# Seven block products for eight in a gate/up projection, on one core

## The chip, the cores and the metric

The kernel runs on one core of a Trainium2 chip. The metric is the device time of one execution in microseconds (us). Three runs of the kernel before took 954.88, 955.64 and 956.01 us; the median is 955.64 us.

## The reference

The kernel computes one decoder layer on x of 512 tokens by 1024 channels in float32: a SwiGLU block, a mixing block (attention and a state space model) and a second SwiGLU block, each between two RMS norms and added to x. The change lies in the last block:

```python
def swiglu(x, w_in, w_out):
    gate, up = jnp.split(x @ w_in, 2, axis=-1)
    return (jax.nn.silu(gate) * up) @ w_out
...
        h = rms_norm(x, ffn2_pre_g[l])
        x = x + 0.5 * rms_norm(swiglu(h, ffn2_w_in[l], ffn2_w_out[l]), ffn2_post_g[l])
```

w_in is 1024 x 5632 (2816 gate columns, then 2816 up columns) and w_out 2816 x 1024.

## The kernel before

The layer runs in three parts (f, m, g in `run`): the first SwiGLU, the mix, the second SwiGLU. Between two parts `boundary` closes the one and opens the next.

Float32 products are made of three matmuls. Each operand is split in a high part of type float32r and a rest: ScalarE casts (L102 for weights, L148 for results), VectorE or GpSimd subtracts (L104, L149). `mm3` multiplies high by high, high by rest and rest by high. All matmuls stand at L129.

In SwiGLU the 2816 hidden columns are 22 tiles f of 128. x lies transposed in SBUF, channels on partitions: `x` unscaled, and `xh`, `xl` times the gain of the norm before. For tile f `products(f)` loads the gate chunk and the up chunk (1024 x 128 each, 512 KB, one DMA on SP's queue into `wraw`), splits each into `whi` and `wlo` (four buffers each; the gate's rest on VectorE, the up's on GpSimd) and runs 8 x 3 matmuls with 512 token columns into a PSUM bank `gu`. `hidden(f)` multiplies both banks by the norm's factor `r` on VectorE (L400, L402), applies Silu to the gate on ScalarE (L401), multiplies (L403) and splits the result into `ah`, `al` at place f % 8 (L148, L149). Tiles 0 and 1 are opened by `boundary` in banks `first`, with matmuls of 256 columns.

In the second SwiGLU `outp_tokens(i)` multiplies six tiles with w_out after tiles 6, 12 and 18, into `yo` banks and then `y`, tokens on partitions; the last four tiles wait for `finish`, with their weights in `tw`, loaded while tiles 18 to 21 run. `finish` multiplies them (`yt`), adds, takes the norm and adds the old x, which `tokens_first` has turned to tokens on partitions by TensorE transposes and kept in SBUF as `xt`. Four token blocks b of 128 are finished in the order 0, 1, 2, 3, the last in three parts.

TensorE runs its matmuls in the order in which the program is written (`fix`); what isn't fixed on the other engines is put in order by the scheduler. Each engine then works off its own row of instructions in order. PSUM has eight banks.

The order of the second SwiGLU around the change:

```python
        for f in range(NF):
            if f >= nfirst:
                products(f)
...
            if last and f in (6, 12, 18):
                outp_tokens(f // 6 - 1)
```

Of the kernel before, what the change touches and what calls it, by code (L numbers as in the profile page):

```python
# [12 lines left out]
ALU = mybir.AluOpType  # L13
# [12 lines left out]
FLAST = ((0, 6), (6, 6), (12, 6))  # L26
QOFF = (0, 128, 384, 768, 1280)
RING = 8
HT = S // 2
H = 8  # L30
E = 64
# [9 lines left out]
class Layer:  # L41
# [323 lines left out]
    def ffn_chunks(self, w_in):  # L365
        return [w_in[c] for c in (0, NF, 1, NF + 1)]

    def ffn(self, n, first, scope, params):
        nc = self.nc
        last = not params  # L370
        w_in, w_out, w_tail = (self.a[n + t] for t in "iot")
        early = scope.enter_context(ExitStack())
        hook = self.tokens_first(scope) if last else self.ssm_params(early)
        o0, _, r, late = first
        if not last:
            y = self.ktiles("y")
# [8 lines left out]
        if self.ahead:  # L385
            between = {(nfirst, 0): {}, (nfirst, 1): {6: lambda: late[0](fixp=self.fix)}, (nfirst + 1, 0): {6: late[1]}}
        else:
            between = {(nfirst, 0): {5: late[0]}, (nfirst, 1): {2: late[1]}}

        def products(f):  # L390
            o[f] = []
            for i, c in enumerate((f, NF + f)):
                w = self.ahead.pop(0) if self.ahead else self.load(w_in[c], (KD, P), pool=i == 1)
                b = self.bank("gu")
                self.mmk(b, w, self.xh, self.xl, hooks=between.get((f, i), other[i]))
                o[f].append(b)

        def hidden(f):
            gt, ut = self.tmp("gt"), self.tmp("ut")
            nc.vector.tensor_tensor(out=gt, in0=o[f][0], in1=r, op=ALU.mult)  # L400
            nc.scalar.activation(out=gt, in_=gt, func=AF.Silu)  # L401
            nc.vector.tensor_tensor(out=ut, in0=o[f][1], in1=r, op=ALU.mult)  # L402
# [16 lines left out]
        def outp_tokens(i):  # L419

            f0, nf = FLAST[i]
            for d in range(2):
                b4 = [self.bank("yo") for _ in range(4)]
                for k in range(nf):
                    if k % 2 == 0:
                        wh, wl = self.load(w_out[(f0 + k) // 2, d], (2, S), pool=k % 4 == 2)
                    s = (f0 + k) % RING
                    for b in range(4):
                        ts = slice(b * P, (b + 1) * P)
                        self.mm3(b4[b], ah(s)[:, ts], al(s)[:, ts], wh[:, k % 2], wl[:, k % 2], k == 0, k == nf - 1)  # L430
                for b in range(4):
                    if i == 0:
                        nc.scalar.copy(out=y(b, d), in_=b4[b])
                    else:
                        nc.vector.tensor_tensor(out=y(b, d), in0=b4[b], in1=y(b, d), op=ALU.add)

        for f in range(NF):
            if f >= nfirst:
                products(f)
            if f == lag:  # L440
                for i in range(lag):
                    hidden(i)
            if f >= lag:
                hidden(f)
            if last and f == 6:
                for _ in hook:
                    pass
                yk = self.ktiles("y")
                y = lambda b, d: yk(2 * b + d)
            if last and f in (6, 12, 18):  # L450
                outp_tokens(f // 6 - 1)
            if not last and f in (7, 14):
                outp(f // 7 - 1)
            if f == NF - NT:
                for _ in hook:
                    pass
                early.close()
                tp = scope.enter_context(self.tc.tile_pool(name="bd" + n, bufs=1))
            if f >= NF - NT:
                self.load_tail(tp, w_tail, f - (NF - NT), f % 2 == 1)  # L460
        tail = lambda k: (ah((NF - NT + k) % RING), al((NF - NT + k) % RING))
        if last:
            return self.finish(y, tail)
        outp(2)
        return y, tail

    def tokens_first(self, scope):

        nc = self.nc
        pool = scope.enter_context(self.tc.tile_pool(name="fin", bufs=1))  # L470
        xt = self.ktiles("xt")
        self.xt = lambda b, d: xt(2 * b + d)
        self.gt = pool.tile([P, 2, S], F32, name="gt")
        nc.sync.dma_start(out=self.gt.rearrange("p d c -> p (d c)"), in_=self.a["glast"].to_broadcast([P, D]))
        for b in range(4):
            for d in range(2):
                yield
                o = self.bank("xt")
                for k in range(4):
                    nc.tensor.transpose(o[:, k * P:(k + 1) * P], self.x(4 * d + k)[:, b * P:(b + 1) * P], self.ident)  # L480
                nc.scalar.copy(out=self.xt(b, d), in_=o)

    def finish(self, y, tail):


        nc, V, fx = self.nc, self.nc.vector, self.fix
# [5 lines left out]
        parts = lambda b: ((0, S), (S, S)) if b < 3 else ((0, S), (S, HT), (S + HT, HT))  # L492
        cols = lambda c, n: (c // S, slice(c % S, c % S + n))

        def product(b, i, k0=0, k1=NT):
# [17 lines left out]

        def gain(b, i):
            d, sl = cols(*parts(b)[i])
            yg[b, i] = self.wp.tile([P, S], F32, name="yg", tag=("whi", "wlo")[b % 2], bufs=4)[:, :parts(b)[i][1]]
# [12 lines left out]

        def final(b, i):  # L530
            c, n = parts(b)[i]
            fx(V.scalar_tensor_tensor(out=yg[b, i], in0=yg[b, i], scalar=rs[:, b:b + 1], in1=at(self.xt, b, i),
                                      op0=ALU.mult, op1=ALU.add))
            fx((nc.scalar if i == 1 else nc.sync).dma_start(out=self.a["out"][b * P:(b + 1) * P, c:c + n], in_=yg[b, i]))

        early = [(0, 0), (0, 1)]
        for b, i in early:
            product(b, i, 0, NT - 1)
        for b, i in early:
            product(b, i, NT - 1)  # L540
        for b in range(1, 4):
            for i in range(len(parts(b))):
                product(b, i)
        for b in range(3):
            for i in range(2):
                gather(b, i)
                gain(b, i)
                add_sum(b, i)
                if i == 0 and b:
                    final(b - 1, 0)  # L550
                    final(b - 1, 1)
        final(2, 0)
        for i in range(2):
            gather(3, i)
            gain(3, i)
        add_sum(3, 0)
        add_sum(3, 1)
        gather(3, 2)
        gain(3, 2)
        add_sum(3, 2)  # L560
        final(2, 1)
        for i in range(3):
            final(3, i)


    def ssm_params(self, scope):
# [599 lines left out]
    def run(self, parts="fmg"):  # L1166
# [5 lines left out]
        for p, q in zip(parts, parts[1:] + " "):  # L1172
            with ExitStack() as scope:
                if p == "m":
                    out = self.mix(first, scope)
                else:
                    out = self.ffn("w1" if p == "f" else "w2", first, scope, p == "f")
                if p != "g":
                    first = self.boundary(*out, *post[p], *nxt[q])

# [66 lines left out]
```

## Time and profile before

| | us |
|---|---|
| median of three runs | 955.64 |
| span of the profiled execution, first to last instruction | 951.7 |
| own time of the profiled execution | not given apart from its span |
| second SwiGLU, from its first matmul to the last one of `finish` | 602.1 to 944 |
| one transfer of 512 KB of w_in from issue to landing (median of 44) | 3.5 |

The span is that of one execution; the runs' median is 3.9 us longer than it, for what lies around the instructions. TensorE's clock was granted at 0.998 on average. In the views below PE is TensorE, PEld its weight loads, DVE VectorE, ACT ScalarE, POOL GpSimd and SP the engine whose queue issues most transfers. In the chain, each row is a piece of work that had to end before the next could start; in the groups, the number behind the bar is the busy time, then the mean time of one.

### The profile page before, as it was taken

Reading aid. Unit: us, or ns where it says so; the run is one execution under the profiler, and the core shown is the slowest. Engines: PE = TensorE matmul, PEld = TensorE weight load, DVE = VectorE, ACT = ScalarE, POOL = GpSimd, SP = SyncE. Lnnn points to the kernel's source line nnn. Section 1 sums busy time; section 2 is a strip of 40 time slices with the busy share of each in tenths; the row PEclk is TensorE's granted clock in tenths of the full one; section 3 lists DMA queues with packets and bytes.
Section 4 is the critical chain, followed back from the end, with each engine's and each line's share of the span. In section 5 each row is a group of like instructions: output and inputs, shape, how many; then the busy total and the mean of one; then the engine's idle time right before and its main releaser. Section 6 shows DMA issues by size and latency. Waiting matters only on the chain.

```text
span 951.7 us, 12868 instructions
## 1 busy us (share of the span) xinstructions
PE 940.0 (99%) x5082; PEld 787.6 (83%) x5082; DVE 527.2 (55%) x934; ACT 367.2 (39%) x610; POOL 225.8 (24%) x134
## 2 busy tenths in 40 slices
PE   9999999999999999999999999999999999999996
PEld 7888888888888889978777899888888888888885
DVE  7998214463255545758897659644134524544327
ACT  7354334352234233525746545443332312223312
POOL 0234222322223233500000035421222222222301
PEclk9999999999999999999999999999999999999999
DMA  7233334353334241282323430323223223233202
GB/s 268 88 111 98 102 111 144 119 177 103 109 112 133 67 155 46 90 224 92 114 68 116 150 110 1 114 86 106 94 93 107 88 89 109 90 111 126 96 1 89
DMA packets 38173, 102.48 MB, mean 108 GB/s; under 512 B 7616, under 2 KB 10944, under 8 KB 37568
## 3 DMA queue, kind: packets, MB, share of 16 engines
q1 hardware_dynamic: 36528, 98.02, 32.0%
q10 hardware_dynamic: 1584, 3.63, 1.0%
q8 instruction: 40, 0.66, 0.3%
q14 instruction: 21, 0.17, 0.1%
HBM read 94.03 MB, written 7.60 MB: 107 GB/s over the span
## 4 chain that ended last, share of the span: by engine, by line
PE 94%; DVE 3%; ACT 1%; issue 1%; DMA 0%; SPq 0%; POOLq 0%; POOL 0%; DVEq 0%; ACTq 0%
PE gu L129 47%; PE yo L129 21%; PE yt L129 6%; PE first L129 6%; PE prj L129 3%; PE prv L129 2%; PE mo L129 2%; PE st L129 1%; PE ys L129 1%; PE gl L129 1%; PE pt L839 1%; PE sc L129 1%; PE pv L129 1%; ACT whi L102 1%; PE rp L129 0%
## 5 line engine op out<-in xcount | busy, mean ns | idle before, releaser
L104 POOL TENSOR_TENSOR wlo<-wraw,whi 128x1024 fp32r<-128x1024 f32 (+2 forms) x62 | 158.5, 2556 | 497.4 <-ACT whi L102 497.3
L102 ACT CAST whi<-wraw 128x1024 fp32r<-128x1024 f32 (+5 forms) x157 | 154.6, 991 | 302.0 <-PE gu L129 121.6
L129 PE MATMUL gu<-xh,whi 128*128 128x512 f32 x656 | 257.6, 393 | 0.0
L129 PE MATMUL gu<-xh,wlo 128*128 128x512 f32 x656 | 255.7, 390 | 0.5 <-DVE wlo L104 0.5
L129 PE MATMUL gu<-xl,whi 128*128 128x512 f32 x656 | 255.3, 389 | 0.0
L104 DVE TENSOR_TENSOR wlo<-wraw,whi 128x1024 fp32r<-128x1024 f32 (+5 forms) x95 | 113.6, 1202 | 121.5 <-ACT whi L102 121.0
L129 PEld LDWEIGHTS gu<-xh,wlo 128*128 128x128 f32 x656 | 123.1, 188 | 26.8 <-DVE wlo L104 1.0
L129 PEld LDWEIGHTS gu<-xh,whi 128*128 128x128 f32 x656 | 123.2, 188 | 25.4 <-issue 0.4
L129 PEld LDWEIGHTS gu<-xl,whi 128*128 128x128 f32 x656 | 123.2, 188 | 25.1
L402 DVE TENSOR_TENSOR ut<-gu,rs 128x512 f32<-128x512 f32 x41 | 28.2, 689 | 102.9 <-PE gu L129 102.8
L149 DVE TENSOR_TENSOR al<-ut,ah 128x512 fp32r<-128x512 f32 x44 | 67.1, 1527 | 25.4 <-ACT ah L148 25.4
L400 DVE TENSOR_TENSOR gt<-gu,rs 128x512 f32<-128x512 f32 x41 | 28.2, 689 | 50.7 <-PE gu L129 50.7
L129 PE MATMUL yo<-ah,whi 128*128 128x512 f32 x144 | 56.0, 389 | 0.0
L129 PE MATMUL yo<-al,whi 128*128 128x512 f32 x144 | 56.0, 389 | 0.0
L129 PE MATMUL yo<-whi,ah 128*128 128x512 f32 x144 | 56.0, 389 | 0.0
L129 PE MATMUL yo<-wlo,ah 128*128 128x512 f32 x144 | 56.0, 389 | 0.0
L129 PE MATMUL yo<-whi,al 128*128 128x512 f32 x144 | 56.0, 389 | 0.0
L129 PE MATMUL yo<-ah,wlo 128*128 128x512 f32 x144 | 56.0, 389 | 0.0
L148 ACT CAST ah<-ut 128x512 fp32r<-128x512 f32 x44 | 27.2, 621 | 62.1 <-DVE ut L403 62.1
L129 PE MATMUL first<-xh,whi 128*128 128x256 f32 (+1 forms) x144 | 43.3, 301 | 0.2 <-ACT xh L151 0.2
L129 PE MATMUL first<-xl,whi 128*128 128x256 f32 (+1 forms) x144 | 42.7, 296 | 0.6 <-DVE xl L152 0.6
L129 PE MATMUL first<-xh,wlo 128*128 128x256 f32 (+1 forms) x144 | 42.5, 295 | 0.0
(194 smaller groups left out, 1406.3 us busy)
## 6 DMA issues: line engine op xcount, KB each, us to landing
wraw<-w2i SPq DMA_DIRECT2D x44, 512.0 KB, 3.5
wraw<-w1i SPq DMA_DIRECT2D x42, 512.0 KB, 3.4
wraw<-w2o SPq DMA_DIRECT2D x18, 512.0 KB, 3.4
wraw<-w1o SPq DMA_DIRECT2D x16, 448.0 KB, 3.4
wraw<-wmi SPq DMA_DIRECT2D x12, 512.0 KB, 3.7
x<-xT SPq DMA_DIRECT2D x8, 256.0 KB, 4.0
w1d<-w1s SPq DMA_DIRECT2D x8, 256.0 KB, 2.7
w2d<-zb SPq DMA_DIRECT2D x2, 1024.0 KB, 4.9
```

The source lines that it names most:

```text
L102: fix(self.nc.scalar.copy(out=hi, in_=raw))
L104: fix(eng.tensor_tensor(out=lo, in0=raw, in1=hi.bitcast(F32), op=ALU.subtract))
L129: i = self.nc.tensor.matmul(*a, **k)
L148: fix(nc.scalar.copy(out=hi, in_=src))
L149: fix(nc.vector.tensor_tensor(out=lo, in0=src, in1=hi.bitcast(F32), op=ALU.subtract))
L400: nc.vector.tensor_tensor(out=gt, in0=o[f][0], in1=r, op=ALU.mult)
L402: nc.vector.tensor_tensor(out=ut, in0=o[f][1], in1=r, op=ALU.mult)
L839: self.fix(nc.tensor.transpose(b[i][:, o:o + P], sc[:, c:c + P], self.ident))
```

## The change

Tiles 0 to 5 of the second SwiGLU stay as they are. Tiles 6 to 21 are taken in eight pairs (f, f + 1). For a pair, the weights are a 2 x 2 matrix of blocks: a11 and a12 are the gate columns of both tiles by the first and the second half of the channels, a21 and a22 the up columns. x is a 2 x 2 matrix b of channel halves by token halves. Every block product has 2 x 4 x 3 matmuls with 256 token columns. Instead of eight block products, seven are made, with sums of blocks: P1 = a11 b11, P2 = a12 b21, P3 = c2 n2, P4 = c1 n1, P5 = c3 t3, P6 = c2' b22 and P7 = a22 t4, where c3 = a11 + a21, c2 = c3 + a22, c1 = a21 + a22 and c2' = c2 + a12 are sums of weights, made for each pair on VectorE, and n1, n2, t3, t4 are signed sums of x, made once (`sums`) and split once (`plain` and `sums`). P1, P3, P5 and P7 add up in one bank (`wx`); ScalarE copies it after P1 (s1) and after P3 (s2). P2 goes to `wy`, P4 and P6 to `wq`, copied after P4 (q). Sums of these give the gate and the up halves; minus signs are put in with the last products (L602).

For the sums x must carry the norm's factors, so `sums` scales it in place; the copy of the old x therefore goes to DRAM (`xd`) and is read again in `finish`. `outp(0)` now follows tile 5; `outp(1)` and `outp(2)` follow the pairs that start at tiles 10 and 16. The weights of the last four tiles are loaded behind the last pair in the program. The last pair is split by token halves, second half first, and `finish` takes the blocks in the order 2, 3, 0, 1.

```diff
+NSTD = 6
+BLOCKS = (2, 3, 0, 1)
...
+                t = self.tmp("xt")
+                nc.scalar.copy(out=t, in_=o)
+                nc.sync.dma_start(out=self.xd[b, :, d], in_=t)
...
+        def sums():
+            for k in range(KD):
+                V.scalar_tensor_tensor(out=self.x(k), in0=self.x(k), scalar=self.g(4, k), in1=r, op0=ALU.mult, op1=ALU.mult)
+            b = lambda i, j: quarter(self.x, i, j)
+            n1, n2 = wsum(), wsum()
+            V.tensor_tensor(out=v4(n1), in0=b(0, 0), in1=b(0, 1), op=ALU.subtract)
+            V.scalar_tensor_tensor(out=v4(n2), in0=v4(n1), scalar=-1.0, in1=b(1, 1), op0=ALU.mult, op1=ALU.subtract)
+            self.split(*tq[0], n2)
...
+        def plain(n1):
+            bh, bl = self.b16("bh", F32R), self.b16("bl", F32R)
...
+            for q, s in enumerate(src):
+                self.split(v4(v(bh, q)), v4(v(bl, q)), s)
...
+        def block(f, up, kh, extra):
+            t = (fin.tile([P, 1024], F32, name="wx", tag="wx", bufs=3) if extra else
+                 self.wp.tile([P, 1024], F32, name="wraw", tag="wraw", bufs=3))
+            src = w_in[f + NF * up:f + NF * up + 2, :, kh * S:(kh + 1) * S].rearrange("f p c -> p f c")
+            nc.sync.dma_start(out=t.rearrange("p (f c) -> p f c", f=2), in_=src)
+            return t
+
+        def cut(t, pool=False):
+            hi, lo = (self.wp.tile([P, 1024], F32R, name=n, tag=n, bufs=4) for n in ("whi", "wlo"))
+            self.wsplit(t, hi, lo, pool)
+            return hi, lo
...
+            def times(bank, w, xb, first):
+                for g in range(2):
+                    for k in range(4):
+                        c, m = slice(k * HT, (k + 1) * HT), slice((4 * g + k) * P, (4 * g + k + 1) * P)
+                        st = first and g == 0 and k == 0
+                        for i, (wi, xi) in enumerate(((0, 0), (0, 1), (1, 0))):
+                            self.mm(bank[:, g * HT:(g + 1) * HT], lhsT=w[wi][:, m], rhs=xb[xi][:, c],
+                                    start=st and i == 0, stop=g == 1 and k == 3 and i == 2, skip_group_check=True)
...
+            times(X, h11, b11, True)
+            s1 = keep(X)
+            a12 = block(f, 0, 1, False)
+            h12 = cut(a12, True)
+            Y = self.bank("wy")
+            times(Y, h12, b21, True)
+            V.tensor_tensor(out=half(gt, 0), in0=p2(Y), in1=p2(s1), op=ALU.add)
+            a21, a22 = block(f, 1, 0, True), block(f, 1, 1, True)
+            c3 = wsum()
+            add(a11, a21, c3)
+            c2 = wsum()
+            add(c3, a22, c2)
+            times(X, cut(c2), n2, False)
+            s2 = keep(X)
+            c1 = wsum()
+            add(a21, a22, c1)
+            Q = self.bank("wq")
+            times(Q, cut(c1), n1, True)
+            q = keep(Q)
+            times(X, cut(c3), t3, False)
+            V.tensor_tensor(out=q, in0=X, in1=q, op=ALU.add)
+            add(c2, a12, c2)
+            times(Q, cut(c2), b22, False)
+            V.tensor_tensor(out=half(gt, 1), in0=p2(Q), in1=p2(s2), op=ALU.add)
+            nc.scalar.activation(out=gt, in_=gt, func=AF.Silu)
+            times(X, cut(a22, True), t4, False)
...
+        for f in range(NSTD, NF, 2):
+            pair(f, *blocks, *tq)
+            if f in (10, 16):
+                outp(f // 6)
```

How this moves instructions is shown at three places. The first is TensorE where one weight chunk gives way to the next. Before, between the gate chunk (bank gu_6555) and the up chunk (gu_6586) of one tile; a row is an instruction, with the tile written, the tiles read (moving or stationary) and the size:

```order
L129 MATMUL gu_6555<-xh_5054,whi_6550 128x512
L129 MATMUL gu_6555<-xl_5055,whi_6550 128x512
L129 MATMUL gu_6555<-xh_5054,wlo_6551 128x512
L129 MATMUL gu_6586<-xh_5054,whi_6581 128x512
L129 MATMUL gu_6586<-xl_5055,whi_6581 128x512
L129 MATMUL gu_6586<-xh_5054,wlo_6582 128x512
```

With the change, between P3 and P4 of the first pair (wsum's split whi_6327 by n2 in tq, then the next split by n1 in bh, bl):

```order
L132 MATMUL wx_6253<-tq_5645,whi_6327 128x256
L132 MATMUL wx_6253<-tq_5646,whi_6327 128x256
L132 MATMUL wx_6253<-tq_5645,wlo_6328 128x256
L132 MATMUL wq_6359<-bh_6046,whi_6360 128x256
L132 MATMUL wq_6359<-bl_6047,whi_6360 128x256
L132 MATMUL wq_6359<-bh_6046,wlo_6361 128x256
```

The three matmuls stand in the same order, half as wide, and a chunk serves 24 of them as before; 768 matmuls of 512 columns are gone and 1344 of 256 have come.

The second place is VectorE in the middle of the projection. Before, one tile's row of five (gate times r, split of a coming chunk, up times r, product, split of the result):

```order
L400 TENSOR_TENSOR gt_6471<-gu_6415,rs_5058 128x512
L104 TENSOR_TENSOR wlo_6551<-wraw_6549,whi_6550 128x1024
L402 TENSOR_TENSOR ut_6472<-gu_6446,rs_5058 128x512
L403 TENSOR_TENSOR ut_6472<-ut_6472,gt_6471 128x512
L149 TENSOR_TENSOR al_5641<-ut_6472,ah_5640 128x512
```

With the change, from P6 of the first pair (gp_6254 takes its bank wq_6359) into the second pair (bank wx_6482) and the sums of the third (wsum_6781):

```order
L596 TENSOR_TENSOR gp_6254<-wq_6359,kp_6355 128x2x256
L107 TENSOR_TENSOR wlo_6557<-wsum_6554,whi_6556 128x1024
L602 SCALAR_TENSOR_TENSOR gp_6254<-kp_6388,gp_6254 128x2x256
L551 TENSOR_TENSOR wsum_6554<-wsum_6554,wraw_6516 128x1024
L602 SCALAR_TENSOR_TENSOR gp_6254<-wx_6253,gp_6254 128x2x256
L107 TENSOR_TENSOR wlo_6590<-wsum_6586,whi_6589 128x1024
L152 TENSOR_TENSOR al_5644<-gp_6254,ah_5643 128x1024
L107 TENSOR_TENSOR wlo_6620<-wsum_6552,whi_6619 128x1024
L551 TENSOR_TENSOR wsum_6781<-wraw_6713,wx_6777 128x1024
L579 TENSOR_TENSOR gp_6483<-wy_6522,kp_6514 128x2x256
L107 TENSOR_TENSOR wlo_6650<-wsum_6554,whi_6649 128x1024
L551 TENSOR_TENSOR wsum_6783<-wsum_6781,wx_6779 128x1024
```

Splits and sums of the pair after stand between the operations that read this pair's banks; each waits in this row for the ones ahead of it. GpSimd keeps two splits per two tiles, now those of a12 and a22.

The third place is VectorE at the end of the last pair. Before, the last tile ahead of the first sum of `finish` (L510):

```order
L402 TENSOR_TENSOR ut_7725<-gu_7699,rs_5058 128x512
L403 TENSOR_TENSOR ut_7725<-ut_7725,gt_7724 128x512
L149 TENSOR_TENSOR al_5641<-ut_7725,ah_5640 128x512
L510 TENSOR_TENSOR y_6072<-yt_7740,y_6072 128x512
L517 TENSOR_TENSOR yg_7860<-y_6072,gt_5767 128x512
```

With the change (wlo_8489 is the third of the four tail weights; wx_8248 the last pair's bank):

```order
L107 TENSOR_TENSOR wlo_8489<-wraw_8490,whi_8488 128x1024
L593 TENSOR_TENSOR kp_8383<-wx_8248,kp_8383 128x512
L596 TENSOR_TENSOR gp_8249<-wq_8354,kp_8350 128x2x256
L602 SCALAR_TENSOR_TENSOR gp_8249<-kp_8383,gp_8249 128x2x256
L602 SCALAR_TENSOR_TENSOR gp_8249<-wx_8248,gp_8249 128x2x256
L152 TENSOR_TENSOR al_5644<-gp_8249,ah_5643 128x2x256 x2
L673 TENSOR_TENSOR y_6056<-yt_8510,y_6056 128x512
```

A tail split now stands between the last pair's operations, and the result is split in two token halves; only the second scalar-tensor-tensor reads the bank of the last product.

More of the change, by code (lines that the diff above doesn't have):

```diff
@@ L28 @@
 RING = 8
+NSTD = 6
+PLACES = [(f"tq{q}{i}", 1) for q in range(3) for i in range(2)] + 3 * [("wsum", 3)]
+BLOCKS = (2, 3, 0, 1)
 HT = S // 2
@@ L384, in ffn @@
         other = ({5: step}, {1: step, 5: step})
[L385 to L388, printed above, removed]
+        between = {(nfirst, 0): {}, (nfirst, 1): {6: lambda: late[0](fixp=self.fix)}, (nfirst + 1, 0): {6: late[1]}}
         def products(f):
@@ L417, in outp @@
                     nc.vector.tensor_tensor(out=y(m), in0=b, in1=y(m), op=ALU.add)
-        def outp_tokens(i):
+        for f in range(NF):
+            if f >= nfirst:
+                products(f)
+            if f == lag:
+                for i in range(lag):
+                    hidden(i)
+            if f >= lag:
+                hidden(f)
+            if f in (7, 14):
+                outp(f // 7 - 1)
+            if f == NF - NT:
+                for _ in hook:
+                    pass
+                early.close()
+                tp = scope.enter_context(self.tc.tile_pool(name="bd" + n, bufs=1))
+            if f >= NF - NT:
+                self.load_tail(tp, w_tail, f - (NF - NT), f % 2 == 1)
@@ L439, in ffn @@
+        for f in range(NSTD):
+            if f >= len(o0) // 2:
                 products(f)
[L440 to L443, printed above, removed]
+            if f == 2:
+                hidden(0)
+                hidden(1)
+            if f >= 2:
                 hidden(f)
-            if last and f == 6:
+            if f == 3:
                 for _ in hook:
                     pass
-                yk = self.ktiles("y")
-                y = lambda b, d: yk(2 * b + d)
@@ L450, in ffn @@
[L450 to L474, printed above, removed]
-        for b in range(4):
[L476 to L481, printed above, removed]
@@ L483, in finish @@
-    def finish(self, y, tail):
-        nc, V, fx = self.nc, self.nc.vector, self.fix
+                n1 = sums()
+        blocks = plain(n1)
+        yk = self.ktiles("y")
+        y = lambda b, d: yk(2 * b + d)
+        outp(0)
+        for f in range(NSTD, NF, 2):
+            pair(f, *blocks, *tq)
+            if f in (10, 16):
+                outp(f // 6)
+        self.tw = []
+        tt = self.b16("tw", F32R).rearrange("p (c i a) b -> p c i (a b)", c=2, i=2)
+        for c in range(NT):
+            self.tw.append([tt[:, c, i] for i in range(2)] if c < 2 else None)
@@ new lines, in swiglu_half, with finish @@
+        for c in range(NT):
+            if c < 2:
+                self.load(w_tail[c], (2 * NT, P), self.tw[c], c % 2 == 1)
+            else:
+                hi, lo = (self.wp.tile([P, 1024], F32R, name=n, tag=n, bufs=4) for n in ("whi", "wlo"))
+                self.load(w_tail[c], (2 * NT, P), [hi, lo], c % 2 == 1)
+                self.tw[c] = [hi, lo]
+        self.finish(fin, y, lambda k: (ah((NF - NT + k) % RING), al((NF - NT + k) % RING)))
+    def finish(self, fin, y, tail):
+        nc, V, fx = self.nc, self.nc.vector, self.fix
+        xt = [self.wp.tile([P, 1024], F32, name="xt", tag="wraw", bufs=3) for b in range(3)]
+        xt.append(fin.tile([P, 1024], F32, name="xt", tag="wx", bufs=3))
+        for b in range(4):
+            self.dma(out=xt[b], in_=self.xd[b].rearrange("p d c -> p (d c)"))
+        xtt = lambda b, d: xt[b][:, d * S:(d + 1) * S]
@@ L515, in gain @@
             d, sl = cols(*parts(b)[i])
-            yg[b, i] = self.wp.tile([P, S], F32, name="yg", tag=("whi", "wlo")[b % 2], bufs=4)[:, :parts(b)[i][1]]
+            yg[b, i] = fin.tile([P, S], F32, name="yg", tag=PLACES[len(yg)][0],
+                                bufs=PLACES[len(yg)][1])[:, :parts(b)[i][1]]
             fx(V.tensor_tensor(out=yg[b, i], in0=at(y, b, i), in1=self.gt[:, d, sl], op=ALU.mult))
```

135 lines of the change are left out of this document (103 added, 32 removed).

## The prediction

> **What bounds the kernel now.** I read the page's head, then the chain of work that ended last in order of time, then the windows, then the groups. The page's head comes first:
>
> ```profile
> span 951.7 us, 12868 instructions
> PE 940.0 (99%) x5082; PEld 787.6 (83%) x5082; DVE 527.2 (55%) x934; ACT 367.2 (39%) x610; POOL 225.8 (24%) x134
> ```
>
> TensorE is busy 99% of the span. Busy time of overlapping matmuls says little about their rate, so the chain follows (start, length, what, count); the changed stretch begins at about 600 us.
>
> ```profile
> 353.50 15.55 PE yt L129 x132
> 569.73 5.46 PE yt L129 x48
> 584.16 10.08 PE first L129 x84
> 661.19 32.64 PE yo L129 x144
> 693.83 65.28 PE gu L129 x288
> 759.11 32.64 PE yo L129 x144
> 791.75 65.28 PE gu L129 x288
> 889.67 32.64 PE gu L129 x144
> 922.31 13.77 PE yt L129 x60
> ```
>
> From 661 us to 936 us the chain is TensorE alone, without a gap. The reader should see two rates. A matmul with 512 moving columns (gu, yo) starts every 65.28 / 288 = 0.2267 us. One with 256 columns starts every 5.46 / 48 = 0.1138 us (yt, the second boundary), 15.55 / 132 = 0.1178 us (yt, the first) or 10.08 / 84 = 0.1200 us (first). So half the columns cost 0.502 to 0.529 of the time. The windows say why it is not always half (start and end, then length, and busy us of PE, PEld, DVE, ACT and POOL, each with its count, granted clock, DMA share, GB/s):
>
> ```profile
> core 0: us, PE busy (x) PEld busy (x) DVE busy (x) ACT busy (x) POOL busy (x), PEclk, DMA share, GB/s
> 584.16:594.24 10.08, 10.08 (x87) 10.08 (x86) 9.90 (x22) 5.46 (x15) 5.45 (x7) 1.00 0.00 0
> 695.00:745.00 50.00, 50.00 (x222) 41.39 (x221) 24.22 (x22) 15.17 (x19) 13.18 (x5) 1.00 0.29 96
> 661.00:700.00 39.00, 39.00 (x173) 32.28 (x172) 7.49 (x8) 13.41 (x17) 7.17 (x3) 1.00 0.27 88
> ```
>
> With 256 columns weights are being loaded the whole time (PEld 10.08 of 10.08); with 512 they are for 41.39 of 50. Both are at full clock. In the changed stretch VectorE works half of the time, ScalarE 30%.
>
> **The change, part by part.** *Removed and added on TensorE.* Tiles 6 to 21 had 16 x 2 x 24 = 768 matmuls of 512 columns, 768 x 0.2267 = 174.1 us. They become 8 pairs x 7 products x 24 = 1344 matmuls of 256 columns: 1344 x 0.1138 = 152.9 us at best, 1344 x 0.1200 = 161.3 us at worst by these rows. By operands the nearest row is first (weights from whi and wlo, halves of x); by the way results gather (12 matmuls in a row into one half bank) it is yt. I take the middle, 0.1178: 158.3 us, so -15.8 us.
>
> The Trainium skill ("TensorE: Matmul & The Clock Gate", sections "LDWEIGHTS (loading the stationary operand)" and "Back-to-back issue gap") speaks against narrow matmuls: a load of 128 weight columns takes 128 / 1.2 = 107 ns however few columns follow it, and a matmul N / 2.4 + 2.5 ns, 109 ns for 256 columns and 216 for 512. By that page, an estimate, the same exchange would be 1344 x 0.109 - 768 x 0.216 = -19 us. The row of first lies 10% above the page's gap, and there the measured row decides.
>
> *VectorE, ScalarE and GpSimd in a pair.* The costs are these (count, busy us, mean ns, then idle before), and below them the timeline around one GpSimd operation and around two earlier ones:
>
> ```profile
> L104 DVE TENSOR_TENSOR wlo<-wraw,whi 128x1024 fp32r<-128x1024 f32 x76 | 99.4, 1312 | 111.2 <-ACT whi L102 111.0
> L532 DVE SCALAR_TENSOR_TENSOR yg<-yg,rs,xt 128x512 f32<-128x512 f32 x7 | 5.1, 745 | 1.1 <-POOL rs L528 1.1
> L104 POOL TENSOR_TENSOR wlo<-wraw,whi 128x1024 fp32r<-128x1024 f32 x50 | 134.9, 2697 | 415.6 <-ACT whi L102 415.5
> L102 ACT CAST whi<-wraw 128x1024 fp32r<-128x1024 f32 x126 | 131.9, 1052 | 244.0 <-PE gu L129 101.7 <-PE yo L129 82.8 <-issue 32.4
> L433 ACT COPY y<-yo 128x512 f32<-128x512 f32 x8 | 4.7, 589 | 5.2 <-PE yo L129 4.6
> L129 PE MATMUL first<-xh,whi 128*128 128x256 f32 x128 | 36.9, 288 | 0.0
> ...
> 700.17 1.23 DVE L104 TENSOR_TENSOR wlo<-wraw,whi 128x1024 fp32r<-128x1024 f32 x1 [0.17 <-ACT whi L102]
> 715.63 0.69 DVE L402 TENSOR_TENSOR ut<-gu,rs 128x512 f32<-128x512 f32 x1 [3.31 <-PE gu L129]
> 716.58 2.80 POOL L104 TENSOR_TENSOR wlo<-wraw,whi 128x1024 fp32r<-128x1024 f32 x1 [8.49 <-ACT whi L102]
> 717.80 2.12 DVE L149 TENSOR_TENSOR al<-ut,ah 128x512 fp32r<-128x512 f32 x1 [0.69 <-ACT ah L148]
> ...
> 73.13 9.24 POOL L104 TENSOR_TENSOR wlo<-wraw,whi 128x1024 fp32r<-128x1024 f32 x2 [8.88 <-ACT whi L102]
> 76.82 0.75 DVE L581 TENSOR_TENSOR pp<-pp,pp 128x256 f32<-128x256 f32 x2
> 77.49 0.68 DVE L400 TENSOR_TENSOR gt<-gu,rs 128x512 f32<-128x512 f32 x1
> 78.09 2.04 DVE L581 TENSOR_TENSOR pp<-pp,pp 128x256 f32<-128x256 f32 x1
> ```
>
> A VectorE operation on two SBUF operands takes 1.23 us for 1024 columns alone. When GpSimd runs (716.58 to 719.38) such an operation waits for its end: al took 2.12 us where an operation of that size takes 0.69. The lower rows show the other direction: VectorE ran two-operand operations back to back, and two GpSimd splits took 9.24 us for the usual 5.4; VectorE was held only after gt, which reads PSUM. I take one rule from these rows: whoever has started keeps SBUF, the other waits, and an operation on PSUM and one SBUF operand is exempt. The Trainium skill ("SBUF — State Buffer", section "SBUF: two separate sides") says the same: the port pair that the two engines share is locked for a whole instruction and the loser blocks.
>
> Per pair VectorE has ten operations of 1024 columns (four sums, five splits, one split of the result: 12.3 us), three on PSUM (2.07 us) and two scalar-tensor-tensor (1.49 us): 15.9 us, against 7 x 24 x 0.1178 = 19.8 us of TensorE. GpSimd has two splits per pair, as before. ScalarE has eight casts of 1.05, three copies of 0.59 and one Silu (about 1.06, an estimate from the cast of that size): 11.3 us.
>
> Sums do not settle a queue, so I walk through a middle pair, t = 0 at its first product, 24 x 0.1178 = 2.83 us each, ends seen 0.22 late (288 ns from start to end where starts are 0.118 apart, and 0.05, an estimate, for the semaphore). Product 6 ends at 16.99, seen at 17.21. VectorE, in its new order: add to gp until 17.90; split of c2 for the next pair (its cast runs until 18.26) until 19.53; first scalar-tensor-tensor (Silu until 19.3) until 20.28; sum c2' until 21.51; second one until 22.26; split of c1 until 23.49; split of the result (cast until 23.35) until 24.72; split of c3 until 25.95; sum c3 of the pair after until 27.18; add to gp until 27.87; split of c2' until 29.10; sum c2 until 30.33. GpSimd's split of a22 (cast until 29.59) gets SBUF now, until 32.72. Then sum c1 until 33.95, split of a11 until 35.18, the add into q until 35.87. At 37.03 product 6 of the next pair ends: the loop closes at TensorE's 19.82 us. What must be in time: ScalarE's copy s1 ends at 24.99, product 3 of the next pair overwrites that bank at 25.48; q is due at 36.81 and done at 35.87; the split of a22 is due at 36.81 and done at 32.72; the sums' splits are 4 to 6 us early. So nothing waits in the walk, with as little as 0.5 us to spare. Bounds: nothing, and 1.2 us a pair (next part); I take 0.3 us, 8 x 0.3 = 2.4 us.
>
> *Preparation.* sums and plain put 8 x 0.745 + 11 x 1.23 = 19.5 us on VectorE and 7 casts, 7.4 us, on ScalarE, between products 3 and the end of the first output product: 2 x 48 x 0.2267 + 32.6 = 54 us, in which VectorE otherwise works 24.22 / 50 of the first 22 us and 7.49 / 39 of the rest, 17 us. It fits; nothing for it. Without that cover it would be 5 us at most (one product's weights late). The first output product now follows tile 5 directly, but reads that tile last of six, 5 x 2.72 us later.
>
> *x by DRAM and the tail.* Each queue entry is one of these:
>
> ```profile
> wraw<-w2i SPq DMA_DIRECT2D x44, 512.0 KB, 3.5
> w1d<-w1s SPq DMA_DIRECT2D x8, 256.0 KB, 2.7
> ```
>
> Eight stores of 256 KB and four loads of 512 KB are added on SP's queue, where weights are loaded products ahead and the DMA share is 0.29; a store that waits for ScalarE holds up weights due 10 us later. Nothing for it; at worst one late chunk, 3.5 us. The weights' bytes are unchanged. The tail's four loads move to the last two pairs: by the walk the last (GpSimd, after product 5's end and a cast) is split 1.5 us before the last product ends. The result's half for blocks 2 and 3 does not need the last product, is done about 1.6 us after its end, and is read by the ninth matmul, at 1.8; the other half has 11 us. The new order of blocks thus covers the split; without it the price is 2 us. The end behind the last matmul has the same operations.
>
> Sum: 951.7 - 174.1 + 158.3 + 2.4 = 938.3 us of span. The runs' median, 955.64, lies 3.9 us above this span; the own time of the profiled execution is not given, so I take the 3.9 as what lies around it: **942.2 us**.
>
> **The rivals.** *GpSimd's split of a22 comes late.* If VectorE leaves no gap after 29.6, as at 73.13, GpSimd gets in only at q's add, 35.2 to 37.6 with the next cast behind it, and product 7 (due 36.81) waits about 1 to 1.2 us in each pair: 955.6 - 15.8 + 8 x 1.2 = 949.4. For it: the rows at 73.13. Against: in the walk VectorE waits for a cast at 31.6, a gap.
>
> *VectorE's queue becomes the bound: slower.* If both GpSimd splits always hold VectorE up in full and each split waits 0.17 for its cast as at 700.17, a pair takes 15.9 + 2 x 2.80 + 6 x 0.17 = 22.5 us against 96 x 0.2267 = 21.76 before: 8 x 0.75 = +6, 961.6. It decides from 21.76 us per pair on. For it: VectorE 80% busy in one order, with PSUM waits in it. Against: in the walk one of the two splits lies where VectorE waits for TensorE.
>
> *The work goes down but not the time.* The rebuilt order has 1344 matmuls for 768, so the work does shrink; no gain would need 174.1 / 1344 = 0.1295 us per matmul, say by weight loads that no longer hide as at 584.16. 955.6. Against: no 256-column row is above 0.120.
>
> *Fast weight loads.* If all run at the second boundary's 0.1138 and nothing waits: 955.6 - 21.2 = 934.4. Against: the first rows, with this kernel's own weights, are at 0.1200, and the walk has 0.5 us to spare at most places. By the matmul gap of the Trainium skill (same page and section as above) this case would go lower still.
>
> **How the numbers follow.** The forecast has 0.63, the fast case 0.07, the late split 0.14, no gain 0.06, VectorE as the bound 0.10. The forecast's own range: 0.115 and no wait gives 955.6 - 174.1 + 154.6 = 936; 0.1200 and 0.9 us a pair give 955.6 - 12.8 + 7.2 = 950. The range takes in the fast case and the late split: 934 to 951. A measurement of this kernel tells about 0.2% from no change, 1.9 us. Faster by more: 0.63 + 0.07 + 0.14 and 0.01 of no gain, 0.85; within: the other 0.05 and 0.01 of VectorE as the bound, 0.06; slower: 0.09.
>
> **What would show it.** Right: groups wx, wy and wq with 1344 matmuls, in the chain in pieces of 24 or more at 0.114 to 0.120 us; a run of three pairs in 57 to 60 us; PE busy in every window of it; VectorE about 80% busy. Wrong: waits of wx, wy or wq for DVE or POOL (lo tiles) or for a kept copy, each over 0.5 us a pair, or a matmul spacing above 0.120. A chain that ends on DVE inside the pairs would mean the slower rival.

## The result, and the profile after

| | before | after |
|---|---|---|
| median of the runs made side by side | 955.26 us (953.89 to 956.01) | 940.31 us (939.08 to 941.10) |
| ratio, 95% interval | | 0.9845 [0.9832, 0.9859] |
| span of the profiled execution | 951.7 us | 937.3 us |
| own time of the profiled execution | not given | 939.08 us |

The changed kernel is 1.55% faster, 15 us; 942.2 was forecast, within 934 to 951. The page's head after:

```profile
span 937.3 us, 14181 instructions
...
PE 925.7 (99%) x5658; PEld 803.6 (86%) x5658; DVE 588.5 (63%) x994; ACT 407.3 (43%) x650; POOL 225.0 (24%) x134
```

TensorE has 576 matmuls more (5658 for 5082) and is 14.3 us less busy (925.7 for 940.0). The chain of work that ended last, in order of time (start us, us, what, count), around the first pair and at the end:

```profile
649.93 32.64 PE yo L132 x144
682.57 2.87 PE wx L132 x24
685.44 2.88 PE wy L132 x24
688.32 2.83 PE wx L132 x24
691.15 2.88 PE wq L132 x24
694.04 2.83 PE wx L132 x24
696.87 2.88 PE wq L132 x24
699.75 5.71 PE wx L132 x48
...
742.62 32.68 PE yo L132 x144
...
908.05 13.65 PE yt L132 x60
```

Each row is one product of a pair (the last one here holds a seventh product and the next pair's first). The chain goes from row to row without a gap, and there are two rates: the four products on plain blocks of x take 2.87 or 2.88 us (0.120 us a matmul), the three on sums of x 2.83 (0.1178). The windows of the two runs of three pairs, of the last two pairs, and of a middle pair alone (window, length, then busy us and count of PE, PEld, DVE, ACT and POOL, granted clock, DMA share, GB/s):

```profile
682.57:742.62 60.05, 60.05 (x506) 60.05 (x505) 38.68 (x39) 31.72 (x37) 15.06 (x6) 1.00 0.30 100
...
775.30:835.35 60.05, 60.05 (x505) 60.05 (x505) 39.50 (x41) 31.24 (x36) 15.07 (x6) 1.00 0.31 101
...
868.00:908.00 40.00, 40.00 (x338) 40.00 (x337) 26.57 (x26) 21.75 (x25) 12.91 (x5) 1.00 0.26 84
...
702.60:722.60 20.00, 20.00 (x170) 20.00 (x170) 14.82 (x16) 10.72 (x13) 5.41 (x2) 1.00 0.30 106
```

Eight pairs take 60.05 + 60.05 + 40.00 = 160.1 us, where 174.1 stood: -14.0 of the -14.4 us between the two spans. The other 0.4 lies ahead of the pairs: the first output product starts at 649.93, where before it started at 661.19 behind one more tile, 48 x 0.2267 = 10.9 us, that is at 650.3. That is less than traces of kernels with the same order up to there differ by (e5_blocks starts it at 651.48), so it need not come from the change. The end is the same: the chain leaves TensorE at 936.1 us before and at 921.7 after, while the last matmuls run on beside it, and from there 951.7 - 936.1 and 937.3 - 921.7 are both 15.6 us.

### The profile page after: what moved, and what is told of

Same layout as the page of the kernel before. It is cut to its first block, busy times and chain, and to the rows that moved or that the text cites. A ratio compares the mean times of both kernels' runs of the same rounds, so it can differ in the third digit from the quotient of the medians.

```text
span 937.3 us, 14181 instructions
## 1 busy us (share of the span) xinstructions
PE 925.7 (99%) x5658; PEld 803.6 (86%) x5658; DVE 588.5 (63%) x994; ACT 407.3 (43%) x650; POOL 225.0 (24%) x134
## 4 chain that ended last, share of the span: by engine, by line
PE 94%; DVE 3%; ACT 1%; issue 1%; DMA 0%; SPq 0%; POOLq 0%; POOL 0%; DVEq 0%; ACTq 0%
PE gu L132 29%; PE yo L132 21%; PE wx L132 10%; PE yt L132 6%; PE first L132 6%; PE wq L132 5%; PE prj L132 4%; PE wy L132 2%; PE prv L132 2%; PE mo L132 2%; PE st L132 1%; PE ys L132 1%; PE gl L132 1%; PE pt L999 1%; PE sc L132 1%
## 5 line engine op out<-in xcount | busy, mean ns | idle before, releaser
L132 PE MATMUL gu<-xh,whi 128*128 128x512 f32 x400 | 158.0, 395 | 0.0
L132 PE MATMUL gu<-xh,wlo 128*128 128x512 f32 x400 | 156.2, 390 | 0.1
L132 PE MATMUL gu<-xl,whi 128*128 128x512 f32 x400 | 155.7, 389 | 0.0
L132 PEld LDWEIGHTS gu<-xh,wlo 128*128 128x128 f32 x400 | 75.1, 188 | 16.4 <-DVE wlo L107 0.6
L132 PEld LDWEIGHTS gu<-xh,whi 128*128 128x128 f32 x400 | 75.1, 188 | 15.3 <-issue 0.4
L132 PEld LDWEIGHTS gu<-xl,whi 128*128 128x128 f32 x400 | 75.2, 188 | 15.1
L132 PE MATMUL wx<-tq,whi 128*128 128x256 f32 x384 | 69.0, 280 | 0.0
L107 DVE TENSOR_TENSOR wlo<-wsum,whi 128x1024 fp32r<-128x1024 f32 x32 | 39.1, 1221 | 35.2 <-ACT whi L105 35.2
L132 PEld LDWEIGHTS wx<-tq,whi 128*128 128x128 f32 x384 | 58.8, 188 | 0.0
L132 PE MATMUL wx<-tq,wlo 128*128 128x256 f32 x192 | 53.6, 279 | 0.0
```

The source lines that it names most:

```text
L107: fix(eng.tensor_tensor(out=lo, in0=raw, in1=hi.bitcast(F32), op=ALU.subtract))
L132: i = self.nc.tensor.matmul(*a, **k)
```

## The experiments

Medians and ratios to the kernel before, run side by side:

| run | what | us, median (lowest to highest) | ratio [95%] |
|---|---|---|---|
| after | the change | 940.31 (939.08 to 941.10) | 0.9845 [0.9832, 0.9859] |
| e1_wide | all but the product | 954.3 (953.28 to 955.62) | 0.9993 [0.9984, 1.0002] |
| e2_eight | eight half-width products | 965.21 (964.35 to 966.38) | 1.0111 [1.0096, 1.0127] |
| e3_vecsplit | GpSimd's splits on VectorE | 940.2 (939.99 to 941.56) | 0.9844 [0.9829, 0.9858] |
| e4_sum1 | one sum twice | 940.91 (940.22 to 941.22) | 0.9847 [0.9832, 0.9862] |
| e4_sum3 | three sums twice | 955.72 (950.03 to 959.10) | 0.9997 [0.9976, 1.0019] |
| e5_blocks | old block order | 941.59 (940.39 to 942.07) | 0.9854 [0.9838, 0.9870] |
| e6_rates | other orders of matmuls | 940.33 (939.31 to 941.15) | 0.9846 [0.9833, 0.9860] |
| e7_place | hi and lo 4 KB apart | 940.95 (940.26 to 942.07) | 0.9854 [0.9841, 0.9868] |
| e8_align | weights moved by 64 bytes | 947.42 (946.2 to 947.5) | 0.9908 [0.9896, 0.9921] |
| e9_four | pairs from tile 4 | 949.46 (949.25 to 949.56) | 0.9934 [0.9920, 0.9947] |
| e10_shift | pairs' operands moved | 937.43 (937.16 to 940.35) | 0.9827 [0.9811, 0.9842] |
| e11_base | the same, all tiles 64 bytes on | 938.44 (938.27 to 939.55) | 0.9839 [0.9825, 0.9853] |

### Is it the product, or what came with it?

e1_wide puts the ordinary tiles back and keeps the other edits:

```diff
-        blocks = plain(n1)
...
-        for f in range(NSTD, NF, 2):
-            pair(f, *blocks, *tq)
+            if f >= len(o0) // 2:
+                products(f)
...
+            if f in (6, 12, 18):
+                outp(f // 6 - 1)
```

> Everything of the change but the product itself: tiles 6 to 21 are again 768 matmuls of 512 columns on the old halves of x, with no sums and no preparation; x by DRAM, the tail's loads behind the loop and blocks 2 and 3 first at the end all stay. My theory (only the matmul count pays, the other edits cost and gain nothing): the time of before, 955.3, within 1.5 us. Rival (part of the 15 us comes from the other edits): 945 to 953. Rival (the other edits cost time that the product pays for): 957 or more.

It took 954.3 us, the interval of the ratio holds 1. x by DRAM, the moved tail and the block order together neither cost nor gain 0.2%; the first theory holds, both rivals fall.

e2_eight keeps the half width and drops the saving:

```diff
-            times(X, cut(c2), n2, False)
...
+                for kh, xs in ((0, (b11, b12)), (1, (b21, b22))):
+                    w2 = cut(block(f, up, kh, up == 1), kh == 1)
+                    for h in range(2):
+                        times(ps[up, h], w2, xs[h], kh == 0)
```

> The pairs compute their eight plain block products with 256-column matmuls, no sums of weights or of x: 8 x 24 = 192 matmuls a pair for 168. My theory (time is matmuls times 0.119 to 0.120 us, nothing else): 8 pairs x 24 matmuls x 0.1195 = 23 us over the changed kernel, 963 (962 to 965), so 8 us slower than before: the halved width alone is a loss, the seventh product alone makes the gain. Rival (the sums, on VectorE, cost time too): less than 20 us over the changed kernel, below 960.

Its chain at the first pair's end and its window of three pairs (columns as above):

```profile
700.62 2.88 PE wx L132 x24
703.50 2.88 PE wy L132 x24
...
683.35:752.46 69.11, 69.11 (x577) 69.11 (x577) 16.01 (x13) 18.27 (x22) 14.49 (x6) 1.00 0.28 92
```

All products are on plain blocks here, all at 0.120: three pairs take 69.11 us against 60.05, and 65.28 for the same six tiles before. VectorE works 16.01 us there where the change has 38.68, and the run still is 24.9 us over the change in the median, where the rival that the sums cost time has less than 20: it falls. 965.21 lies just above the expected 962 to 965. Half width alone loses 3.8 us per three pairs; the seventh-for-eighth product wins 9.1, of which some 0.4 is that three of the seven run at 0.1178 in place of 0.120.

### How near is VectorE's queue to being the bound?

e3_vecsplit hands both of GpSimd's splits to VectorE:

```diff
-            h12 = cut(a12, True)
+            h12 = cut(a12)
...
-            times(X, cut(a22, True), t4, False)
+            times(X, cut(a22), t4, False)
```

> The two splits of a pair that GpSimd does (a12, a22; 2.4 us each) go to VectorE: 2 x 1.23 us more on it, 18.4 of the 20.0 us of a pair by the prediction's count, and no lock between the two engines. My theory (neither queue bounds the pairs): 940.3 within 1.5 us. Rival (GpSimd's hold on SBUF cost time): faster by over 2 us. Rival (VectorE's queue is nearly the bound): slower, 2 to 10 us.

940.2: no change, and both rivals fall. The change left nothing to win back, since its trace shows no wait of TensorE from 603 to 940 us; and without GpSimd's splits beside it, VectorE has room for 2.46 us more.

e4_sum1 and e4_sum3 leave GpSimd its splits and load VectorE by computing sums twice into the same tile:

```diff
             add(a11, a21, c3)
+            add(a11, a21, c3)
...
             add(c3, a22, c2)
+            add(c3, a22, c2)
...
             add(a21, a22, c1)
+            add(a21, a22, c1)
```

(e4_sum1 has the last of the three only.)

> One sum of weights per pair (c1) is computed twice, the second time over the first: 1.22 us more on VectorE in each pair, nothing else. My walk had 0.5 us to spare at its tightest place, the copy of the first product's bank; the trace shows 1.4 us there (the copy ends at 726.95, the product starts at 728.36). By the trace: at most 0.3 us a pair, 940 to 943. By the walk: 0.7 us a pair, 946.

> Three sums of weights per pair (c3, c2, c1) are computed twice: 3.7 us more on VectorE in each pair, 15.9 + 3.7 = 19.6 us by the prediction's count, and GpSimd's two splits of 2.4 us that share SBUF with it. My theory (the rival of the prediction, VectorE as the bound, becomes real here): a pair takes 21 to 23 us instead of 20.0, 948 to 964. Rival (VectorE still hides, since GpSimd works only where VectorE waits): 940 to 943.

One sum more: 940.91, no change that can be told, and not the walk's 946; one wait of 0.3 us, for the add into a kept bank, is all that its trace shows in the pairs. Three sums more: 955.72 in the median, the whole gain gone. The chain of e4_sum3 at the starts and ends of the runs of pairs, and within the first; then its list of PE's waits (total us, times, longest) and a window:

```profile
683.51 2.87 PE wx L132 x24
...
697.80 2.78 PE wq L132 x23
700.65 1.06 ACT whi L105
701.73 1.00 DVE wlo L107
702.88 0.68 DVE gp L605
703.56 1.14 DVE wsum L551
...
719.74 3.32 DVE wsum L551
723.06 0.61 DVE kp L596
723.72 5.98 PE wx L132 x48
...
779.51 2.87 PE wx L132 x24
...
819.72 7.48 PE wx L132 x48
...
844.34 32.68 PE yo L132 x144
```

```profile
PE wx L132 <- DVE kp L596: 6.0, 2, 3.0
PE wx L132 <- POOL wlo L107: 1.7, 1, 1.7
```

```profile
683.51:746.83 63.32, 60.31 (x505) 60.10 (x505) 51.61 (x45) 31.93 (x37) 17.03 (x6) 1.00 0.29 96
```

The reader sees the chain leave TensorE for VectorE inside the pairs, from 700.65 to 723.06, and come back with a wait of 3.0 us for the add into q, whose turn comes behind the doubled sums. Runs of three take 63.32 and 844.34 - 779.51 = 64.83 us for 60.05, so some 21.3 us a pair, in the expected band. This is the prediction's slower rival, made real.

That does not account for the whole median. The trace is of the fastest of ten executions, 950.03 us, and its span is 948.2 - 937.3 = 10.9 us longer than that of the change. The other nine take up to 959.10, and the longest of them show the lowest mean granted clocks, down to 0.989 where this one has 0.996. What one stop can do to the clock stands in this trace: after the first stop of 3.0 us the clock stays at 1.00 and the next 48 matmuls take 5.98 us (5.71 in the change); after the second, equally long, it is 0.50 from 821 to 824 us, and they take 7.48. That the slower executions have more of the same is likely, but no trace of them shows it.

The queue thus bounds the pairs from somewhere between 1.2 and 3.7 us more work a pair on; the change itself lies below that.

### The end, and the preparation

e5_blocks sets the old order of token blocks:

```diff
-BLOCKS = (2, 3, 0, 1)
+BLOCKS = (0, 1, 2, 3)
```

> The end takes the token blocks in their old order (0, 1, 2, 3) instead of 2, 3, 0, 1, so that its first matmuls read the result of the last product. The prediction's price for that: 2 us, 942.3. Rival (something else hides it): 940.3 within 0.5. Rival (split and activation are longer in the way): 944 or more.

Its chain at the end:

```profile
909.60 1.40 PE yt L132 x6
911.04 12.81 PE yt L132 x54
```

The sixty matmuls take 911.04 + 12.81 - 909.60 = 14.25 us for 13.65: TensorE loses 0.6 us in this trace, not 2. The median, 1.3 us higher, has an interval that overlaps with the change's. The cover is real, its price was put three times too high.

e9_four starts the pairs at tile 4 and takes the preparation's cover away:

```diff
-FLAST = ((0, 6), (6, 6), (12, 6))
+FLAST = ((0, 4), (4, 6), (10, 8))
...
-NSTD = 6
+NSTD = 4
...
-            if f in (10, 16):
-                outp(f // 6)
+            if f in (8, 16):
+                outp(f // 8)
```

> The pairs begin at tile 4 in place of 6 (nine pairs; the output products take tiles 0 to 3, 4 to 9 and 10 to 17), so the preparation has no ordinary tiles in front of it and only the first output product beside it, 96 x 0.2267 = 21.8 us, for some 19.5 us of VectorE behind tile 3's own 2.7 us and before the first pair's splits. By TensorE's work alone: one pair more, 20.0 for 21.8 us, 938.5. If the preparation's cover is what made it cost nothing: up to the prediction's 5 us of waiting come back, 939 to 944.

Its longest PE wait, and its windows at that place (columns as above):

```profile
PE yo L132 <- DVE wlo L107: 8.8, 1, 8.8
```

```profile
637.00:650.00 13.00, 4.19 (x18) 3.15 (x17) 13.00 (x12) 7.96 (x11) 3.11 (x1) 0.73 0.03 13
650.00:662.14 12.14, 12.14 (x49) 9.91 (x48) 8.47 (x6) 2.81 (x4) 3.83 (x1) 0.86 0.44 139
```

949.46, worse than either expectation: VectorE is busy with the preparation for all of 637 to 650, the first output product's own weight split stands behind it in its queue, and TensorE stops for 8.8 us in one piece. The stop lasts from 640.6 to 649.4 us; the matmuls ahead of it still start every 0.227 us. Behind it the granted clock is 0.50 until 653 us and 1.00 from 654 on (0.86 in the mean of the second window): the nine matmuls from 649.39 take 3.96 us until 653.35, where 9 x 0.2267 = 2.04 would do, so 1.9 us more. 8.8 + 1.9 - 1.75 for the ninth pair = 9.0. The span grew by 947.4 - 937.3 = 10.1, of which 1.5 lie ahead of all that the edit touches (the first matmuls behind the second boundary's yt start at 576.71 for 575.22), so 8.6 are left to explain. The Trainium skill ("TensorE: Matmul & The Clock Gate", section "What's actually happening") has the array drop to half clock after about 3.4 us without work; this run agrees, with 0.50 after 8.8 us. In the change, with two more tiles ahead, the same work costs nothing (no wait of TensorE from 603 to 940 us in its trace): its cover is needed, and the prediction's "5 us at most" without it was too low.

### What sets 0.120 and 0.1178?

e6_rates gives each pair another order of its 24 matmuls per product (half banks in turn, lo of x first, all hi-hi first, and so on):

```diff
+            var = (f - NSTD) // 2
+            pat = [(0, 0), (0, 1), (1, 0)]
+            if var == 1:
+                seq = [(g, k, i) for k in range(4) for i in range(3) for g in range(2)]
+            if var == 2:
+                pat = [(0, 1), (0, 0), (1, 0)]
+            if var == 3:
+                seq = [(g, k, i) for g in range(2) for i in range(3) for k in range(4)]
...
```

> Each of the eight pairs issues its 24 matmuls of a product in another order (pair 0 as it is; 1: the two half banks in turn; 2: lo of x first; 3: all hi-hi, then all hi-lo, then all lo-hi of a half bank; 4: every second k backwards; 5: both; 6: half banks in turn by k; 7: hi-hi, lo-hi, hi-lo). If the spacing of 0.118 to 0.120 us hangs on which operand changes from one matmul to the next, some pairs show 0.113 and end up to 1.1 us earlier. If it hangs on the narrow moving operand alone (weights load the whole time), all eight stay at 0.118 to 0.120 and the time is 940.3 within 1 us.

Second products of its pairs 0, 1 and 2 in its chain:

```profile
686.49 2.88 PE wy L132 x24
...
706.51 2.88 PE wy L132 x24
...
726.53 2.88 PE wy L132 x24
```

No product moved in any of the eight pairs. The order of operands and half banks is not it.

e7_place puts hi and lo of a plain block side by side:

```diff
-            bh, bl = self.b16("bh", F32R), self.b16("bl", F32R)
+            b2 = [self.b16(n, F32R).rearrange("p (q k) c -> p q (k c)", q=4) for n in ("bh", "bl")]
...
+                hi, lo = (b2[q // 2][:, 2 * (q % 2) + i] for i in range(2))
```

> The hi and lo part of each plain block of x lie 4 KB apart in one tile, as those of the sums do, where they lay 16 KB apart in two. If the distance of the two makes 0.120 us of 0.118 in the products on plain blocks: 4 products x 24 x 8 x 0.002 = 1.5 us faster than the changed kernel, 938.8. If it is something else: 0.120 stays and 940.3.

940.95, and its products on plain blocks still take 2.88. The distance of hi and lo is not it.

e8_align moves the weights by 64 bytes against x, and two of the sums. Distances in SBUF here and below are worked out from the sizes of the tiles; no trace shows an address.

```diff
+        pool("gap", 1).tile([P, 16], F32, name="gap")
         self.wp = pool("wp", 2)
...
+            if q:
+                fin.tile([P, 24], F32, name="shift", tag=f"shift{q}", bufs=1)
```

> Only places in SBUF change: 64 bytes of nothing ahead of the weight tiles move whi and wlo against the plain blocks of x (their distance was a multiple of 512 bytes and is now 448 modulo 512), and 96 bytes of nothing ahead of the second and the third pair of sum tiles take the distance of these from whi to 416 and to 0 modulo 512 (the first stays at 320, as all three were). If that distance makes the two spacings: the products on plain blocks go from 0.120 to 0.118, the one on the third sum from 0.118 to 0.120, together 8 x 24 x (4 - 1) x 0.002 = 1.2 us less, 939. If something else does: every product keeps its spacing, 940.3.

Its chain: a row of first, for which the change has 10.08; two rows of ordinary tiles and output products, for which the change has 28.77 and 32.64; two products on plain blocks from the first pair; a whole pair later on, but for its last product; and the last product of a run:

```profile
395.49 9.54 PE first L133 x84
...
632.13 29.39 PE gu L133 x126
661.53 32.98 PE yo L133 x144
...
697.33 2.83 PE wy L133 x24
...
708.66 2.73 PE wq L133 x24
...
786.09 2.75 PE wx L133 x24
788.84 2.72 PE wy L133 x24
791.55 2.83 PE wx L133 x24
794.38 2.73 PE wq L133 x24
797.11 2.81 PE wx L133 x24
799.92 2.75 PE wq L133 x24
...
841.55 2.86 PE wx L133 x24
```

From the second pair on each product answers to its move: the plain blocks fall from 2.88 to 2.72 to 2.75, further than expected, as the row of first does (10.08 to 9.54); the sum left alone stays at 2.83 (row 791.55); the one at 416 takes 2.81 (797.11); the one brought to distance 0 rises to 2.86 (841.55). So where the operands lie does change the spacing. It is not all that sets it: in the first pair the plain blocks lie no differently, yet they take 2.83 at first (697.33) and 2.73 only from 708.66 on. And the run is 7 us slower than the change, since the 512-column matmuls, which shared that distance, went the other way: 29.39 / 126 = 0.2333 for 28.77 / 126 = 0.2283, and the first output product starts 11.6 us later (661.53 for 649.93).

e10_shift moves the operands of the pairs alone, e11_base also all large tiles by 64 bytes:

```diff
-        return self.big.tile([P, KD, S], dt, name=name, tag="b16")
+        t = self.big.tile([P, KD * S + 128], dt, name=name, tag="b16p", bufs=2)
+        at = 112 if name in ("bh", "bl") else 0
+        return t[:, at:at + KD * S].rearrange("p (k c) -> p k c", c=S)
...
+        fin.tile([P, 32], F32, name="shift", tag="shift", bufs=1)
         tq = [[fin.tile([P, 1024], F32R, name="tq", tag=f"tq{q}{i}") for i in range(2)] for q in range(3)]
```

> Weight tiles and x keep their distance (0 modulo 512 bytes), so that 512-column matmuls stay at 0.2267; only the operands of the pairs move: the plain blocks and all three sums lie 448 modulo 512 bytes from whi (they were at 0 and 320). If the distance of moving operand and weights sets the spacing of 256-column matmuls, as the run before shows it for the plain blocks (2.72 us for 24, 0.1133), all seven products take 2.72: 8 x (4 x 0.16 + 3 x 0.11) = 7.8 us less than the changed kernel, 932.5. If only the place of the weights themselves counts (they are unmoved here): 940.3. If the sums are different: 5.1 us less, 935.2.

> As the run before (operands of the pairs 448 modulo 512 bytes from whi), and 64 bytes of nothing ahead of all large tiles, so that every distance stays and only the places change: weights and x lie at 32 modulo 128 in place of 96, the operands of the pairs at 96 in place of 32. That is how the plain blocks lay in the run that showed 2.72 us for 24. If the place decides beside the distance: 2.72 in the pairs, 8 x 7 x 0.11 = 6 us less than in the run before, 931.5, unless the 512-column matmuls turn slow as in that run (0.233, and 945 or more). If only the distance decides: 937.4 as before.

A window of three pairs of e10_shift (columns as above):

```profile
682.91:742.27 59.36, 59.36 (x505) 59.36 (x505) 38.80 (x39) 31.70 (x37) 15.10 (x6) 1.00 0.30 102
```

All seven products now take 2.83, 0.1178 (59.36 / 504): no longer 0.120, but not 0.1133. Eight pairs take 8 x 59.36 / 3 = 158.3 us for 160.1. At 937.43 us this version is the fastest here, ratio 0.9827 [0.9811, 0.9842] to the kernel before; against the change its intervals overlap, and the trace's 1.8 us is what stands firm. e11_base has 2.83 as well and 938.44, so the place by itself did not bring 0.1133 back. None of the three times expected of e10_shift, 932.5, 940.3 or 935.2, was met.

Two rows that no move separates show that the place alone does not set the spacing, the 48 matmuls of yt at the second boundary. In the changed kernel:

```profile
569.76 5.46 PE yt L132 x48
```

In e9_four:

```profile
571.06 5.66 PE yt L132 x48
```

Up to there the two kernels are written alike and lay out the same tiles; 0.1138 and 0.1179 us are both spacings of the same stream. e4_sum1, laid out the same, has 5.66 as well. What chooses between the two, and whether the first pair of e8_align, e10_shift and e11_base simply stay at the slower one, stays open.

## Why the prediction was right, point by point

- **TensorE alone is the chain.** Right: the chain goes through the pairs without a gap, and PE is busy in all of every window. A run of three pairs takes 60.05 us, at the edge of the 57 to 60 that were to show it.
- **The rate, 0.1178, 158.3 us.** The right mechanism and nearly the right size: 0.1191 on the mean, 160.1 us. Four of seven products ran at the rate of the row of first, 0.1200, three at the middle value. That the middle came so near is partly luck: it was taken between first, nearest by its operands, and yt, nearest by the way results gather, and that way does not matter (e6_rates). The plain blocks behaved as first in the change and in e8_align, where both became faster; yt shows 0.1138 and 0.1179 at one and the same place. By the gap that the Trainium skill gives for an isolated matmul ("TensorE: Matmul & The Clock Gate", section "Back-to-back issue gap"), 109 ns, the pairs would take 146.5 us, an estimate; the trace has 160.1, and no run came under 0.113.
- **Waits in the pairs, 0.3 us each, 2.4 us.** Too much: none. The walk's order was right but its tightest place was wider. These are rows of the timeline of after, of ScalarE and of GpSimd (start, us, instruction, idle before and releaser):

```profile
726.37 0.58 ACT L565 COPY kp<-wx 128x512 f32<-128x512 f32 x1
```

```profile
712.27 3.00 POOL L107 TENSOR_TENSOR wlo<-wx,whi 128x1024 fp32r<-128x1024 f32 x1 [11.96 <-ACT whi L105]
```

  The copy of the first product's bank ends at 726.95, and the product that overwrites the bank starts at 728.36: 1.4 us to spare where the walk had 0.5. GpSimd's split of a22 ends at 715.27 and is due at 719.77, 4.5 us early (walk: 4.1); its 3.00 us for 2.40 fits VectorE holding SBUF, as the rule from before's rows had it (a sum of two SBUF tiles, begun at 711.77, ends at 712.99). e4_sum1 shows that 1.2 us more still fits.
- **Preparation and x by DRAM, nothing.** Right: for x by DRAM e1_wide shows it, for the preparation, which e1_wide leaves out, the trace of the change, without a wait of TensorE beside it. Without its cover the preparation costs 8.8 us of waiting and more in clock (e9_four), not 5 at most.
- **The tail, nothing; without the block order 2 us.** The first half right; the price is 0.6 us of TensorE (e5_blocks).
- **The sum.** Forecast span 938.3, measured 937.3: +1.8 of rate, -2.4 of waits, -0.4 ahead of the pairs. So two errors of 2 us with opposite signs nearly cancel, and that the span came within 1.0 us is partly luck. Of the 1.9 us between 942.2 and 940.31 the other 0.9 is what was taken to lie around the span: 3.9, where the median after lies 940.31 - 937.3 = 3.0 above it. The profiled execution's own time, 939.08, lies 1.8 above its span, so part of the 3.9 was the median lying above that execution.
- **The rivals.** Late a22 split: not seen, 4.5 us early. VectorE as the bound: not here, but real with 3.7 us more a pair (e4_sum3). No gain: 0.1295 was not reached. Fast weight loads: not here; e8_align shows 0.1133 to 0.1146 on the four products on plain blocks, so the rate exists.
- **VectorE about 80% busy.** 14.82 of 20.00 in the middle pair, 74%, and 64% over a run of three, whose third pair prepares no next one.

## What to carry to other kernels

When TensorE is the whole chain, a product that needs one multiplication in eight less is worth its count times the measured spacing, and the narrower width must be charged first: here 9.1 us won and 3.8 lost per three pairs. The sums come free only as long as the vector engine's queue has room, so load that queue on purpose once to learn where it ends: 1.2 us a pair was free, 3.7 us cost 10.9 us in the fastest execution and the whole gain in the median one, since stops of TensorE can also lower its clock. One-off preparation needs enough TensorE work ahead of it, and other engines' small urgent jobs must not stand behind it in a queue.

## What was not expected of the hardware

- The spacing of 256-column matmuls changes with where the moving operand lies against the weights in SBUF: 0.120 us at a distance of 0 modulo 512 bytes (0.119 for the sum that e8_align brought there), 0.117 to 0.118 at 320 and 416, and at 448 once 0.1133 to 0.1146 (e8_align behind its first pair) and twice 0.1178 (e10_shift, e11_base). The place does not decide alone: the same stream at the same place took 0.1138 in one execution and 0.1179 in another (yt, after and e9_four). The order of operands (e6_rates) and the distance of hi from lo (e7_place) made no difference. The rule behind it was not found.
- 512-column matmuls answered the other way: moving the weights by 64 bytes against x took a row of ordinary tiles from 0.2283 to 0.2333 a matmul, and such matmuls in the whole kernel cost more than the pairs gained.
- One stop of TensorE of 8.8 us halved the granted clock for some 4 us behind it (e9_four); of two stops of 3.0 us one did so and one did not (e4_sum3).
